# A two-layer diffusion backbone on one core: the MLPs with six banks, another order of stores, loads and norms, and one more product straight to x

## The chip, the cores and the metric

The kernel runs on one core of a Trainium2 chip. The metric is the device time of one execution in microseconds, the median of several runs.

## The reference

A block of 1024 latent tokens `x` and 256 context tokens `ctx`, 1024 channels wide, go through two layers. Layer 0 is a mixer (Fourier and a state space scan), layer 1 differential attention. Each is followed by an MLP of width 4096. The part that matters here:

```python
def rmsnorm(x, g):
    xf = x.astype(F32)
    y = xf * lax.rsqrt(jnp.mean(xf * xf, axis=-1, keepdims=True) + EPS)
    return (y * g.astype(F32)).astype(x.dtype)

def modulate(h, shift, scale):
    return h * (1.0 + scale) + shift

def adaln(cond, w, b):
    m = jax.nn.silu(cond) @ w + b
    return jnp.split(m[..., None, :], 6, axis=-1)

def sq_relu_mlp(h, w1, w2):
    return jnp.square(jax.nn.relu(h @ w1)) @ w2

# in layer i, behind the mixer or the attention
x = x + g2 * sq_relu_mlp(modulate(rmsnorm(x, norm2_g[i]), sh2, sc2), mlp_w1[i], mlp_w2[i])
if not last:
    ctx = ctx + cg2 * sq_relu_mlp(modulate(rmsnorm(ctx, norm2_g[i]), csh2, csc2), mlp_w1[i], mlp_w2[i])
```

Layer 1 has no MLP for the context. Its modulations `adaln` need a product with a 1024 x 6144 matrix `ada_w`, once for the latent condition and in part for that of the context.

## The kernel before

All of x stays in SBUF with channels on partitions (`xL` for the 1024 latent tokens, `xC` for the context). Tokens are worked in three blocks: columns 0 to 511 and 512 to 1023 of the latents (named by 0 and 512) and the context (`SEQ`, 256 columns). Every fp32 operand of a product is kept as a high and a low half, made by `split` (L337: ACT casts the high half, POOL or DVE subtracts for the low one); `mm3` (L341 to L343) adds three matmuls, high by high, high by low, low by high.

**Products with w1** (`up`). The 32 column groups f of w1 are streamed (`Stream`, loads at L149 on SP's queue into a ring R of raw tiles, splits by ACT and POOL). A product of one f and one block is 8 x 3 matmuls into one PSUM bank, taken in turn from `self.bank(0, 1)`. ACT then reads the bank with relu (L1581) and squares in place. Two neighbouring f make a pair u. When all blocks of a pair are there, `results` makes seven combinations for a seven-product scheme of 2 x 2 blocks (and one for the context): T = C12 - C11 on DVE in a buffer E, then others; each is split by `keep` into a place of the buffer M and stored to DRAM (`h_w`, L1539, SP's queue). `keeps`, called at k = 0, 3 and 6 of each product, takes one step of it. The blocks of the last pair, f = 30 and 31, are taken in the order 0, 512, SEQ.

**Background work.** `self.step(n)` after each product takes n steps of a queue of generators. In the first MLP the queue holds `ada_dve(1)`: 24 chunks of 256 columns of layer 1's `ada_w`. A chunk is loaded in two tiles into ring R (L544, SP's queue), DVE multiplies and adds 8 k-slices into Y (line L296 for all fused operations; 16 operations for the first 8 chunks, which serve both conditions, then 8), and TensorE sums over the partitions (L526). `self.flush()` ends what is left.

**Products with w2.** For c of 0 to 6, q of 0, 1, j of 0 to 6, two products with combined weights (`down_weights`, made on DVE, ACT and POOL), with operands fetched back from `h_w` into slots by POOL's queue (L1604). Products j = 1, 5, 6 go from the bank straight to x by `to_x`, x += gate * bank. The others (0, 2, 3, 4) are summed over c in M by DVE; at c = 6, `together` combines them with POOL additions and adds to x. The last pair of w1 groups, u = 14 and 15 of w2, is multiplied plainly (`last`): block 0 and the context for each d, and then block 512.

**Norms.** `hook(t0, n, d, i)` is called when a channel tile d of a block is final. For a block in `at_once` it squares on ACT and sums on DVE or POOL at once; for others it is done later, in the steps between. The sum over partitions is at L392, its spreading over the partitions at L406. The projections of the attention follow the first MLP, with operands `hl` (latents) and `hc` (context).

In the second MLP there are only two blocks, no `ada` work, and four result places in M.

## Time and profile before

| | |
|---|---|
| median of 3 runs | 3011.8 us (3011.11 to 3018.55) |
| profiled execution | 3013.48 us, span 3011.7 us |
| PE busy | 2815.6 us, 93% |
| DVE busy | 1967.2 us, 65% |
| POOL busy | 1559.2 us, 52% |
| ACT busy | 1131.9 us, 38% |
| DMA | 504.58 MB, mean 168 GB/s |
| mean granted clock of TensorE | 0.97 |

The times in the rows are counted from the start of the span. The products with w1 of the first MLP lie at about 490 to 1055 us, those with w2 until about 1480, the attention's projections from 1492. The second MLP runs from about 2333 to the end. A line number with an engine is the line of the code that issued the instruction; many DVE operations go through one helper (L296), so the operands' names tell them apart. A wait is put down to the engine and line that released it last.

### The profile page before, as it was taken

The numbers are of one execution on the slowest core, as the hardware profiler recorded it, in microseconds if no ns is written. First come the engines' busy times: TensorE is split into PE (matmuls) and PEld (weight loads), VectorE is DVE, ScalarE is ACT, GpSimd is POOL, SyncE is SP. The second block draws the span as 40 slices with busy tenths as digits, with TensorE's granted clock in tenths as the row PEclk, the third lists the DMA queues.
The fourth block names the chain that finished last, engine by engine and source line by source line (L and its number), as shares of the span: only waits on it lengthen the run. The fifth ranks groups of instructions, "written<-read, shape, count | busy, mean of one in ns | idle before, by whom it ended". The sixth has DMA issues, their size and how long they took to land.

```text
span 3011.7 us, 40545 instructions
## 1 busy us (share of the span) xinstructions
PE 2815.6 (93%) x14850; PEld 2342.4 (78%) x14850; DVE 1967.2 (65%) x3694; ACT 1131.9 (38%) x2036; POOL 1559.2 (52%) x1282
## 2 busy tenths in 40 slices
PE   5899999888888889999789999999999999999999
PEld 2666788777777778888667878999988888877887
DVE  7889877555333445557648893999986543446666
ACT  3342343333333321111323443666653544532220
POOL 5613233433343465667524442777751555667775
PEclk8898999999999899999999999999999999999999
DMA  7265530555555785856126454232313465589882
GB/s 288 85 188 167 193 102 8 189 182 199 206 203 204 245 248 172 254 170 196 60 97 168 131 136 136 84 95 76 109 36 119 148 235 203 222 278 290 251 248 82
DMA packets 304358, 504.58 MB, mean 168 GB/s; under 512 B 17568, under 2 KB 175776, under 8 KB 303648
## 3 DMA queue, kind: packets, MB, share of 16 engines
q1 hardware_dynamic: 235344, 355.18, 35.4%
q0 software_dynamic: 68816, 146.82, 16.3%
q8 instruction: 117, 1.92, 0.3%
q14 instruction: 81, 0.66, 0.1%
HBM read 332.56 MB, written 169.38 MB: 167 GB/s over the span
## 4 chain that ended last, share of the span: by engine, by line
PE 68%; DVE 12%; DMA 7%; issue 5%; ACT 4%; POOL 3%; SPq 0%; DVEq 0%; POOLq 0%; ACTq 0%
PE bank L341 17%; PE bank L343 16%; PE bank L342 16%; DMA R<-in_ada_w_dram 4%; PE sc L1957 4%; PE pv L1997 4%; DVE Y L296 4%; PE tb L1988 2%; DVE E L296 2%; DVE S L296 1%; PE sc L342 1%; PE sc L343 1%; PE sc L341 1%; POOL M L337 1%; DVE hl L296 1%
## 5 line engine op out<-in xcount | busy, mean ns | idle before, releaser
L337 POOL TENSOR_TENSOR W<-R,W 128x512 fp32r<-128x512 f32 (+1 forms) x196 | 341.1, 1750 | 509.9 <-ACT W L333 501.9
L341 PE MATMUL bank<-hl,W 128*128 128x512 f32 (+1 forms) x1224 | 490.7, 401 | 70.2 <-ACT M L1581 61.5
L342 PE MATMUL bank<-hl,W 128*128 128x512 f32 (+1 forms) x1224 | 482.4, 394 | 5.5 <-DVE hl L296 5.5
L343 PE MATMUL bank<-hl,W 128*128 128x512 f32 (+1 forms) x1224 | 479.9, 392 | 1.0 <-DVE W L337 1.0
L341 PE MATMUL bank<-hb,W 128*128 128x512 f32 x968 | 381.8, 394 | 3.2 <-ACT W L333 1.7
L343 PE MATMUL bank<-hb,W 128*128 128x512 f32 x968 | 379.7, 392 | 1.3 <-POOL W L337 1.3
L342 PE MATMUL bank<-hb,W 128*128 128x512 f32 x968 | 377.4, 390 | 0.0
L341 PEld LDWEIGHTS bank<-hl,W 128*128 128x128 f32 x1224 | 238.3, 195 | 141.8 <-ACT M L1581 64.4
L333 ACT CAST W<-R 128x512 fp32r<-128x512 f32 (+2 forms) x237 | 184.7, 798 | 303.2 <-PE bank L343 157.3
L342 PEld LDWEIGHTS bank<-hl,W 128*128 128x128 f32 x1224 | 238.3, 195 | 52.9 <-DVE hl L296 9.8
L343 PEld LDWEIGHTS bank<-hl,W 128*128 128x128 f32 x1224 | 237.2, 194 | 50.2 <-DVE W L337 1.4
L296 DVE SCALAR_TENSOR_TENSOR xL<-bank,k,xL 128x512 f32<-128x512 f32 x232 | 171.6, 747 | 133.5 <-PE bank L343 130.3
L296 DVE SCALAR_TENSOR_TENSOR Y<-R,k,Y 128x256 f32<-128x256 f32 x224 | 152.4, 713 | 102.2 <-DMA R<-in_ada_w_dram 99.0
L343 PEld LDWEIGHTS bank<-hb,W 128*128 128x128 f32 x968 | 182.0, 188 | 43.5 <-POOL W L337 2.1
L341 PEld LDWEIGHTS bank<-hb,W 128*128 128x128 f32 x968 | 182.2, 188 | 43.0 <-ACT W L333 2.5
L342 PEld LDWEIGHTS bank<-hb,W 128*128 128x128 f32 x968 | 182.2, 188 | 40.0 <-issue 0.2
L1962 DVE TENSOR_REDUCE S<-sc 128x1 f32<-128x1280 f32 x128 | 184.2, 1479 | 38.9 <-PE sc L1957 38.9
L296 DVE TENSOR_TENSOR M<-bank,M 128x512 f32<-128x512 f32 x192 | 131.2, 689 | 105.5 <-PE bank L343 105.4
L337 POOL TENSOR_TENSOR W<-E,W 128x512 fp32r<-128x512 f32 x112 | 144.9, 1312 | 98.6 <-ACT W L333 98.4
L1581 ACT ACTIVATE M<-bank 128x512 f32<-128x512 f32 (+1 forms) x160 | 88.4, 553 | 264.4 <-PE bank L343 264.3
L1957 PE MATMUL sc<-K,W 128*128 128x512 f32 x720 | 168.1, 370 | 0.0
L324 POOL TENSOR_TENSOR R<-R,S 128x896 f32<-128x896 f32 x64 | 107.3, 1677 | 111.2 <-DVE S L296 94.2
(405 smaller groups left out, 6488.5 us busy)
## 6 DMA issues: line engine op xcount, KB each, us to landing
h_w<-M SPq DMA_DIRECT2D x228, 512.0 KB, 3.1
hl<-h_w POOLq DMA_DIRECT2D x106, 512.0 KB, 7.5
hb<-h_w POOLq DMA_DIRECT2D x106, 512.0 KB, 7.7
R<-in_w_dram SPq DMA_DIRECT2D x64, 512.0 KB, 4.1
R<-in_w_dram SPq DMA_DIRECT2D x112, 256.0 KB, 4.6
R<-in_ada_w_dram SPq DMA_DIRECT2D x52, 512.0 KB, 4.3
W<-q_d POOLq DMA_DIRECT2D x15, 1024.0 KB, 5.4
A<-in_ada_w_dram SPq DMA_DIRECT2D x24, 512.0 KB, 4.7
```

The lines of the kernel that those rows point to most:

```text
L296: f(**kw)
L324: self.nc.gpsimd.tensor_tensor(out=o, in0=a, in1=b, op=op)
L333: nc.scalar.copy(hi, src)
L337: e.tensor_tensor(out=lo, in0=src, in1=hi.bitcast(F32), op=ALU.subtract)
L341: mm(ps, lhsT=lh, rhs=rh, start=first, stop=False)
L342: mm(ps, lhsT=lh, rhs=rl, start=False, stop=False)
L343: mm(ps, lhsT=ll, rhs=rh, start=False, stop=last)
L1581: nc.scalar.activation(out=e, in_=ps, func=AF.Relu)
L1957: nc.tensor.matmul(self.SC[i][:, c0:c0 + n], lhsT=Qf[:, e, q0:q0 + 128], rhs=K[:, i, c0:c0 + n], start=e == 0, stop=e == 1)
L1962: nc.vector.tensor_reduce(out=st[:, i, 1:2], in_=self.SC[i][:, 0:1280], axis=AX.X, op=ALU.max, negate=True)
L1988: nc.tensor.transpose(ps[:, 128 * j:128 * j + 128], it["P"][0][:, 128 * (c0 + j):128 * (c0 + j) + 128], self.ident)
L1997: nc.tensor.matmul(self.PV[:, 0:128], lhsT=it["wT"][:, kt], rhs=heads[h]["v"][:, kt], start=kt == 8, stop=kt == 3)
```

## The change

Both MLPs are changed, by parts:

- `up` takes its bank from six in turn, not two.
- A store of a result is issued one `keep` later (`held`).
- `Stream.lean`, set in the first MLP: after a split the next raw load is issued only if none is waiting.
- `step` after a product takes 2 and 3 steps in turn.
- The last pair's blocks are taken in the order SEQ, 0, 512 in the first MLP, and the context's first operands are fetched right behind the context's products.
- For the plainly multiplied pair, every second split of w2 has its subtraction on DVE.
- Product j = 4 goes straight to x twice (512 of d and of 4 + d); M needs 12 places, `together` two additions.
- At the end of the first MLP the context's `hook` comes after that of block 512, and block 512's squares are summed at once.
- The second MLP has three result places; its x-hat of block 512 lies in `oS`, whose other half gives 8 free slots, and Y serves for a part of M (`Halves`).

```diff
 class Stream:
-        self.extra, self.depth, self.turn = [], 2, 0
+        self.extra, self.depth, self.turn, self.lean = [], 2, 0, False
...
-        self.load()
+        if not self.lean or self.nl <= self.ns:
+            self.load()
...
-                self.split(a, w[:, 0].rearrange("p a b -> p (a b)"), w[:, 1].rearrange("p a b -> p (a b)"), elo="p")
+                self.split(a, w[:, 0].rearrange("p a b -> p (a b)"), w[:, 1].rearrange("p a b -> p (a b)"),
+                           elo="v" if u > 13 and i % 2 else "p")
...
-        turn = ([10, 12, 14] if ctx else [8, 10, 12, 14]) * 50
+        turn = ([10, 12, 14] if ctx else [8, 10, 12]) * 50
...
+        held = []
...
-                t = turn.pop(0) if u < 15 else (12, 14)[i % 2]
-                o = duo(t)
+                o = duo(turn.pop(0) if u < 15 else ((12, 14) if ctx else (12, 10))[i % 2])
                 self.split(src, o[:, 0].bitcast(F32R), o[:, 1].bitcast(F32R), elo=elo)
-                nc.sync.dma_start(out=fl(hd)[u, i], in_=o.rearrange("p a b -> p (a b)"))
+                if held:
+                    held.pop(0)()
+                held.append(lambda: nc.sync.dma_start(out=fl(hd)[u, i], in_=o.rearrange("p a b -> p (a b)")))
...
         def up(f, w, t0, n, beside):
-            ps, (hh, hl), u = self.bank(0, 1)[:, :n], self.hv(t0, n), f // 2
+            ps, (hh, hl), u = self.bank(0, 1, 2, 3, 4, 5)[:, :n], self.hv(t0, n), f // 2
...
-            self.step(2)
+            count[2] += 1
+            self.step(2 + count[2] % 2)
...
             if k % 3 == 0 and done:
                 if next(done[0], 0) == 0:
                     done.pop(0)
+            elif k % 3 == 0 and held:
+                held.pop(0)()
...
-        free = [None]
-        for t0, n in blocks:
+        free, last_up = [None], blocks[2:] + blocks[:2]
+        for t0, n in last_up:
...
-            if t0 != blocks[-1][0]:
+            if t0 == SEQ:
+                fetch_ctx(0)
+            elif t0 == 0:
                 fetch_free(*free)
         self.ws.done(2)
         make(6)
-        fetch_ctx(0)
         fetch_free(*free)
...
-        M = [{(0, 0): 0, (0, 1): 1, (2, 0): 2, (2, 1): 3, (3, 0): 8, (3, 1): 9, (4, 0): 10, (4, 1): 11},
-             {(0, 0): 4, (0, 1): 5, (2, 0): 6, (2, 1): 7, (3, 0): 12, (3, 1): 13, (4, 0): 14, (4, 1): 15}]
+        M = [{(0, 0): 0, (0, 1): 1, (2, 0): 2, (2, 1): 3, (3, 0): 8, (3, 1): 9},
+             {(0, 0): 4, (0, 1): 5, (2, 0): 6, (2, 1): 7, (3, 0): 10, (3, 1): 11}]
+        TO = {1: [(0, 0)], 4: [(0, 512), (4, 512)], 5: [(0, 512)], 6: [(4, 0)]}
...
-                        if j in (1, 5, 6):
-                            to_x(ps, dh if j == 6 else dl, 512 if j == 5 else 0)
+                        if j in TO:
+                            for d, t0 in TO[j]:
+                                to_x(ps, d + 2 * q + e, t0)
...
                 last(w, d, t0, n)
-                hook(t0, n, d, i)
+                if t0 < SEQ:
+                    hook(t0, n, d, i)
...
+            for i, d in enumerate(self.LAST):
+                hook(SEQ, CTX, d, i)
...
-        hook = self.norm_hook(1, 0, pool=True, wait=(3, 3))
+        hook = self.norm_hook(1, 0, (0, 512), pool=True, wait=(3, 3))
...
+        self.ws.lean = True
         self.mlp(0, MIX, slots, sc, ready, hook, before)
+        self.ws.lean = False
...
-        slots = [(None, hb2.v(6, 2, 512)[:, i]) for i in range(6)] + [(0, v0[:, :, i]) for i in range(8)] + \
-                [(512, v1[:, :, i]) for i in range(8)]
+        slots = [(t0, a[:, :, i, o:o + 512]) for t0, a, o in ((None, oS, 512), (0, v0, 0), (512, oS, 0))
+                 for i in range(8)]
```

Three places of the new order follow. The numbers behind a name are those of its buffers; a line of the changed kernel is 16 to 29 higher than the same one before.

TensorE at the end of the w1 products of the first MLP. Before, the last context product of f = 29, four sums over the partitions of ada chunks, and the first product of the last pair:

```order
L343 MATMUL bank1_1_61<-hc_50_3828,W12_53_7688 128x256
L526 MATMUL bank1_7_67<-k_7_94,Y53_21_7899 128x1 x2
L526 MATMUL bank1_7_67<-k_7_94,Y53_22_7998 128x1 x2
L526 MATMUL bank1_7_67<-k_7_94,Y53_23_8014 128x1 x2
L526 MATMUL bank1_7_67<-k_7_94,Y53_24_8030 128x1 x2
L341 MATMUL bank1_0_60<-hl_47_3675,W12_54_7782 128x512
```

Changed, the last of all these sums, six products earlier than there (W12_51 is the weight of f = 27, W12_52 that of f = 28):

```order
L359 MATMUL bank1_5_65<-hc_50_3828,W12_51_7539 128x256
L542 MATMUL bank1_7_67<-k_7_94,Y53_24_7720 128x1 x2
L357 MATMUL bank1_0_60<-hl_47_3675,W12_52_7637 128x512
L358 MATMUL bank1_0_60<-hl_47_3675,W12_52_7637 128x512
L359 MATMUL bank1_0_60<-hl_47_3675,W12_52_7637 128x512
```

The last sum has moved in front of f = 28's products, and no sum stands between the loop and the last pair.

POOL's queue around the last product with w1, before (hl_47 and hl_48 are slots of block 0 and 512, hc_50 those of the context; W12 are weights for w2):

```order
L1604 DMA hl_47_3675<-h_w0_4555 128x2x512 x6
L1604 DMA hl_48_3679<-h_w0_4555 128x2x512 x4
L1604 DMA hl_47_3675<-h_w0_4555 128x2x512 x2
L1604 DMA hl_48_3679<-h_w0_4555 128x2x512 x4
L337 TENSOR_TENSOR W12_57_8255<-E14_189_8059,W12_57_8255 128x512
L337 TENSOR_TENSOR W12_57_8255<-E14_190_8060,W12_57_8255 128x512
L337 TENSOR_TENSOR W12_58_8261<-E14_188_8058,W12_58_8261 128x512
L337 TENSOR_TENSOR W12_58_8261<-E14_189_8059,W12_58_8261 128x512
L1604 DMA hc_50_3828<-h_w0_4555 128x2x512 x4
```

Changed:

```order
L1627 DMA hc_50_3828<-h_w0_4555 128x2x512 x2
L1627 DMA hl_47_3675<-h_w0_4555 128x2x512 x6
L353 TENSOR_TENSOR W12_57_8247<-E14_189_8059,W12_57_8247 128x512
L353 TENSOR_TENSOR W12_57_8247<-E14_190_8060,W12_57_8247 128x512
L353 TENSOR_TENSOR W12_58_8253<-E14_188_8058,W12_58_8253 128x512
L353 TENSOR_TENSOR W12_58_8253<-E14_189_8059,W12_58_8253 128x512
L1627 DMA hl_48_3679<-h_w0_4555 128x2x512 x4
L1627 DMA hl_47_3675<-h_w0_4555 128x2x512 x2
L1627 DMA hl_48_3679<-h_w0_4555 128x2x512 x4
L1627 DMA hc_50_3828<-h_w0_4555 128x2x512 x2
```

The first two fetches of hc have moved from behind the four splits of W12 to the front, and the fetches into hl_48 from in front of the splits to behind them.

DVE at the end of the first MLP, where Y53 holds the sums of squares (256 columns for the context, 512 for a latent block) and the writes of xL are the last products' additions to x. Before:

```order
L337 TENSOR_TENSOR hl_47_3675<-E14_243_11395,hl_47_3675 128x512
L296 SCALAR_TENSOR_TENSOR hl_47_3675<-E14_244_11413,k_9_102,hl_47_3675 128x512
L296 TENSOR_TENSOR Y53_28_11419<-Y53_28_11419,E14_245_11421 128x256
L296 SCALAR_TENSOR_TENSOR xL_37_2870<-bank1_2_62,k_9_102,xL_37_2870 128x512
L296 TENSOR_TENSOR Y53_28_11419<-Y53_28_11419,E14_246_11442 128x256
L296 TENSOR_TENSOR Y53_28_11419<-Y53_28_11419,E14_247_11445 128x256
L296 TENSOR_TENSOR Y53_28_11419<-Y53_28_11419,E14_248_11448 128x256
L296 TENSOR_TENSOR Y53_28_11419<-Y53_28_11419,E14_249_11451 128x256
L296 TENSOR_TENSOR Y53_28_11419<-Y53_28_11419,E14_250_11454 128x256
L296 TENSOR_TENSOR Y53_28_11419<-Y53_28_11419,E14_251_11457 128x256
L296 SCALAR_TENSOR_TENSOR xL_37_2870<-bank1_3_63,k_9_102,xL_37_2870 128x512
```

Changed:

```order
L312 SCALAR_TENSOR_TENSOR E14_249_11447<-xL_37_2870,k_10_106,Y53_28_11356 128x512
L353 TENSOR_TENSOR hl_47_3675<-E14_247_11426,hl_47_3675 128x512
L312 SCALAR_TENSOR_TENSOR hl_47_3675<-E14_249_11447,k_9_102,hl_47_3675 128x512
L312 SCALAR_TENSOR_TENSOR xL_37_2870<-bank1_2_62,k_9_102,xL_37_2870 128x512
L312 TENSOR_TENSOR Y53_27_11295<-Y53_27_11295,E14_248_11445 128x512
L312 SCALAR_TENSOR_TENSOR xL_37_2870<-bank1_3_63,k_9_102,xL_37_2870 128x512
L312 TENSOR_TENSOR Y53_27_11295<-Y53_27_11295,E14_250_11472 128x512
L312 TENSOR_TENSOR Y53_27_11295<-Y53_27_11295,E14_251_11488 128x512
L353 TENSOR_TENSOR W12_122_11491<-R13_153_11456,W12_122_11491 128x512 x2
```

The last addition to xL has come ahead of the context's sums, which no longer stand here; sums of block 512 stand in their place, one ahead of it and two behind.

## Rows read from the trace of the kernel before

**Rows 1.** Busy time of each engine by stage; then granted clock, DMA share, GB/s.

```profile
490.00:1080.00 590.00, 508.23 (x2532) 432.67 (x2531) 276.92 (x469) 211.44 (x373) 240.73 (x170) 0.92 0.56 193
1080.00:1440.00 360.00, 357.48 (x1903) 308.81 (x1902) 215.68 (x315) 68.80 (x116) 242.81 (x234) 1.00 0.68 202
1440.00:1560.00 120.00, 93.25 (x403) 73.15 (x404) 67.37 (x119) 38.22 (x70) 49.05 (x38) 0.89 0.17 52
```

**Rows 2.** Waits of PE, 480 to 1090: total us, times, longest us.

```profile
PE bank L341 <- ACT M L1581: 63.6, 16, 6.5
PE bank L341 <- DMA hc<-h_w: 9.5, 2, 9.2
PE bank L526 <- DVE Y L296: 8.8, 4, 3.4
```

**Rows 3.** Timeline of PE after a wait: start, us, what [idle before <-releaser].

```profile
726.38 0.79 PE L341 MATMUL bank<-hl,W 128*128 128x512 f32 x1 [4.57 <-ACT M L1581]
726.97 0.63 PE L342 MATMUL bank<-hl,W 128*128 128x512 f32 x1
727.40 0.63 PE L343 MATMUL bank<-hl,W 128*128 128x512 f32 x1
...
733.57 0.40 PE L342 MATMUL bank<-hl,W 128*128 128x512 f32 x1
733.80 0.39 PE L343 MATMUL bank<-hl,W 128*128 128x512 f32 x1
```

**Rows 4.** Timeline of DVE around the same wait.

```profile
722.30 1.67 DVE L296 SCALAR_TENSOR_TENSOR Y<-R,k,Y 128x256 f32<-128x256 f32 x4 [4.62 <-DMA R<-in_ada_w_dram]
723.89 0.68 DVE L296 TENSOR_TENSOR E<-M,E 128x512 f32<-128x512 f32 x1
...
725.10 4.73 DVE L296 SCALAR_TENSOR_TENSOR Y<-R,k,Y 128x256 f32<-128x256 f32 x4
```

**Rows 5.** Timeline of ACT around the same wait.

```profile
724.65 0.62 ACT L333 CAST M<-E 128x512 fp32r<-128x512 f32 x1 [6.16 <-DVE E L296]
...
725.74 0.59 ACT L1581 ACTIVATE M<-bank 128x512 f32<-128x512 f32 x1
```

**Rows 6.** Timeline of POOL around the same wait.

```profile
725.35 1.35 POOL L337 TENSOR_TENSOR M<-E,M 128x512 fp32r<-128x512 f32 x1 [5.49 <-ACT M L333]
```

**Rows 7.** Waits of DVE, 480 to 1060: total us, times, longest us.

```profile
DVE Y L296 <- DMA R<-in_ada_w_dram: 206.0, 41, 9.1
```

**Rows 8.** Busy time of DVE, 560 to 750.

```profile
560.00:750.00 190.00, 107.06 (x172) 0.92 0.56 196
```

**Rows 9.** Timeline of POOL at the end of the w1 stage.

```profile
1056.32 5.41 POOL L337 TENSOR_TENSOR W<-E,W 128x512 fp32r<-128x512 f32 x4 [0.41 <-ACT W L333]
1061.67 2.87 POOL L1604 DMA_DIRECT2D hc<-h_w  x4
```

**Rows 10.** Waits of PE, 1080 to 1560.

```profile
PE bank L341 <- DVE xL L296: 14.3, 2, 12.9
PE bank L341 <- ACT hl L333: 5.3, 3, 4.1
PE bank L406 <- DVE E L296: 4.2, 2, 3.0
PE bank L392 <- DVE Y L296: 2.7, 1, 2.7
PE bank L341 <- DVE M L296: 1.5, 2, 0.8
```

**Rows 11.** Timeline of DVE at the end of the first MLP.

```profile
1485.85 4.47 DVE L296 TENSOR_TENSOR Y<-Y,E 128x256 f32<-128x256 f32 x5
...
1491.12 0.74 DVE L296 SCALAR_TENSOR_TENSOR xL<-bank,k,xL 128x512 f32<-128x512 f32 x1
```

**Rows 12.** Waits of PE in the second MLP's w1 stage, 2330 to 2690.

```profile
PE bank L341 <- ACT M L1581: 1.5, 1, 1.5
```

**Rows 13.** Waits of ACT in that same stage.

```profile
ACT M L333 <- DMA h_w<-M: 33.0, 28, 3.0
```

More of the change, by code (lines that the diff above doesn't have):

```diff
@@ L95, in v, with __init__, free @@
         return self.places.pop(0)
+class Halves:
+    def __init__(self, b):
+        self.b, self.i = b, 1
+    def v(self, *shape):
+        self.i ^= 1
+        return self.b.v(*shape, o=self.b.n // 2 * self.i)
+    def free(self):
+        self.b.free()
 class Alt:
@@ L1505, in mlp @@
         ctx = len(order) == 3
-        mem = [self.buf("M", 6144)]
+        mem = [self.buf("M", 6144, side="L" if ctx else "R")]
         def duo(i):
@@ L1516, in mlp @@
         fl = lambda a: a.bitcast(F32)
-        turn = ([10, 12, 14] if ctx else [8, 10, 12, 14]) * 50
+        turn = ([10, 12, 14] if ctx else [8, 10, 12]) * 50
         total = (14 * 8 + 16) if ctx else (14 * 7 + 8)
-        gen, Wq, count = self.down_weights(layer, ctx, 1 + ctx), [], [0, -1]
+        gen, Wq, count = self.down_weights(layer, ctx, 1 + ctx), [], [0, -1, 0]
         def make(k=1):
@@ L1668, in together @@
             q, e = divmod(dp, 2)
-            m = {j: place(M[q][j, e]) for j in (0, 2, 3, 4)}
+            m = {j: place(M[q][j, e]) for j in (0, 2, 3)}
             to_x(m[0], dp, 0)
@@ L1673, in together @@
             self.ptt(m[3], m[2], m[3], ALU.add)
+            to_x(m[2], dp, 512)
             yield
             to_x(m[3], dp + 4, 0)
-            self.ptt(m[2], m[2], m[4], ALU.add)
             yield
-            to_x(m[2], dp, 512)
-            self.ptt(m[4], m[3], m[4], ALU.add)
-            yield
-            to_x(m[4], dp + 4, 512)
+            to_x(m[3], dp + 4, 512)
             yield
@@ L1706, in mlp @@
                     for e in range(2):
-                        ps, dl, dh = bank(), 2 * q + e, 4 + 2 * q + e
+                        ps = bank()
                         for p in range(2):
@@ L1728, in mlp @@
                         keeps(0)
+                        if j == 6:
+                            while done or held:
+                                keeps(0)
                     if c == 6 and q:
@@ L1754, in mlp @@
             self.go(g)
-        for r in mem:
+        for r in mem[:1 + ctx]:
             r.free()
@@ L2153, in hook @@
                 if i == 0:
-                    acc[t0] = [self.Y.v(n) for _ in range(2 if pool else 1)]
+                    acc[t0] = [self.Y.v(n) for _ in range(2 if pool and t0 == 0 else 1)]
                 for add in left.pop(t0, []):
@@ L2328, in second @@
         self.Kr.free()
[L2329 to L2331 removed]
+        hb0 = b("hb0", 2 * 8 * 512, True)
+        v0, v1 = hb0.v(2, 8, 512), oS[:, :, :, 0:512]
+        self.hx_views([v0[:, 0], v0[:, 1]], [v1[:, 0], v1[:, 1]])
         for _ in gen:
             pass
[L2334 to L2337 removed]
         self.ws.eng = ("a", "p")
@@ L2343, in put @@
             nc.sync.dma_start(out=self.out[:, d, t0:t0 + n], in_=self.xL.v(8, SEQ)[:, d, t0:t0 + n])
-        slots = [(None, hb2.v(6, 2, 512)[:, i]) for i in range(6)] + [(0, v0[:, :, i]) for i in range(8)] + \
-                [(512, v1[:, :, i]) for i in range(8)]
+        slots = [(t0, a[:, :, i, o:o + 512]) for t0, a, o in ((None, oS, 512), (0, v0, 0), (512, oS, 0))
+                 for i in range(8)]
         self.mlp(1, LAT, slots, (), None, put, lambda t0, n: self.flush_norm(t0))
-        for h in (hb2, hb1, self.Y, hb0):
+        for h in (hb0, self.Y, oSb):
             h.free()
```

11 lines of the change are left out of this document (2 added, 9 removed).

## The prediction

> **What bounds the kernel now.** I first read the busy shares by stage [rows 1], because the mean over the program hides where TensorE stands still. From 490 to 1080 us (first MLP, products with w1) PE is busy 508.23 of 590 us at a mean granted clock of 0.92. In the products with w2 that follow, 1080 to 1440, it is busy 357.48 of 360 at 1.00. From 1440 to 1560, the end of that MLP and the start of the attention projections, it is busy 93.25 of 120 at 0.89. In the other MLP, PE waits 1.5 us in all of its w1 stage [rows 12], with the same two banks. So there are two holes, some 82 us of waiting and some 27, each with a slow clock beside it. The rest that the change touches runs at TensorE's pace.
>
> Next I read who is waited for. In the first hole: 63.6 us in 16 waits for ACT's relu of an earlier product (its bank isn't read yet), 9.5 for the fetch of hc, 8.8 in four waits for the sums of the ada steps [rows 2]. That is 81.9, the whole hole. One of the 16 shows the chain [rows 3 to 5]. DVE gives E, the difference that ACT must cast, at 723.89; ACT casts it at 724.65 after 6.16 us of waiting, and the relu that PE needs stands behind it on ACT's queue and runs at 725.74. PE starts at 726.38, 4.57 us late. So the relus aren't slow (0.59 us). They queue behind a cast that waits for DVE, and with two banks PE can be only one product ahead. DVE is late since it waits for the ada weights, 206.0 us in 41 waits [rows 7], in order with the rest of its work.
>
> After that wait PE's starts lie 0.43 us apart (726.97 to 727.40), later 0.23 (733.57 to 733.80) [rows 3]: the two clock levels, 1.2 and 2.4 GHz. The clock was at the lower one when PE came out of the wait.
>
> **Six banks in the w1 stage.** A 512-column product is 24 matmuls x 0.23 = 5.5 us. PE may now run five products ahead instead of one, so ACT may be 4 x 5.5 = 22 us later than before without PE noticing. The longest wait was 6.5 [rows 2], three in a row would still fit, and ACT, busy 211.44 of 590 us [rows 1], catches up. Gone: 63.6, less about 5 (estimated) for the first of the 16, where the block's norm, whose making isn't changed, would be late next. Gain 58.6; at least 37 if ACT's delays add up and the 22 us are won only once.
>
> **Ada steps denser.** `step` is called with 2 or 3 per product instead of 2; most of the sums on PE now come every third product instead of every fourth. The four sums that stood behind the loop, 8.8 us [rows 2], come before its end: gain 8.8. But DVE must do a chunk in less time. The stretch 560 to 750 holds 8 chunks of 16 operations with DVE busy 107.06 [rows 8]. About 24 of the 190 us are PE's waits (the hole's 13% share) and 15 its clock of 0.92, so the same PE work lasts about 151. It then carries 10.7 chunks. A step takes 0.42 or 1.18 us (below), 0.73 with POOL busy 41% of the time [rows 1]; 107.06 + 2.7 x 16 x 0.73 = 139 of 151 us, 92% of DVE. PE waits for a sum directly, so lateness is now a gap. DVE in time gives 0; the longest wait of this kind before, 3.4 us [rows 2], on each of the eight heavy chunks gives 27. I take 14. The other 16 chunks have half the operations, and PE's products hide them; without that cover they cost as much again, 14.
>
> Four fused ada steps took 1.67 us at 722.30 with POOL idle, and 4.73 at 725.10 with POOL at work from 725.35 [rows 4, 6]: 0.42 against 1.18 each. The Trainium skill (GPSIMD Engine Reference, 1. Specifications) says that GpSimd shares its SBUF interfaces with VectorE and contends with VectorE instructions that have two SBUF inputs. By that rule DVE work packed closer beside the same POOL work gets dearer, and the time would be rival 2's; the trace agrees on the mechanism, and not yet on the amount.
>
> **Last pair by blocks, fetch of hc early.** hc's fetch stood behind four POOL splits of weights (5.41 us from 1056.32), was issued at 1061.67 [rows 9], and PE waited 9.2 [rows 2]. It is now issued ahead of them, after the context's products, whose buffer it takes: 9.5 gone. Late next are the operands of j = 3, whose fetch now stands behind the same four splits, so at about 1061.7. PE gets to j = 3 after six products of 6 x 0.23 us and four context parts of half that, 11 us. The old wait met PE some 3 us after its last w1 product, this one 8 us later with the same issue time. Between 0 and the old 9.2 I take 4. Net 5.5.
>
> **The clock.** 590 us at 0.92 is 47 us of full-clock work lost [rows 1], over 21 waits or so. I count nine waits left (the norm, seven at ada sums, j = 3), so 47 x 12/21 = 27 would return; part of the slow time lay inside the waits and is counted already, so I take 20, from 10 to 40.
>
> The Trainium skill (TensorE: Matmul & The Clock Gate, A second HAM failure mode: psum-queue depth-cycling) speaks against this: in one kernel, cycling through PSUM banks in each iteration let the clock swing, which is rival 5 here. The w2 stage cycles through six banks at 1.00 and the w1 stage swings with two [rows 1], so the trace doesn't bear it out.
>
> **Order at the end of the MLP.** The first projection waits 12.9 us for a bank that DVE's last addition to x frees [rows 10]. That addition, 1491.12, stands on DVE behind six sums of the context's norm, from 1485.85 on [rows 11]. They move behind it: 1491.12 - 1485.85 = 5.3 gained. The waits of 5.3, 4.2 and 2.7 [rows 10] belong to the second block's norm, which came behind the context's and now comes first; I leave 4 of these 12.2, gain 8.2. j = 4 no longer adds to M, so the 1.5 for M [rows 10] goes too. The clock of 0.89 lost 13 of 120 us [rows 1]; with about half of the waits gone I take 5. Sum 20, from 7 (only the bank) to 30.
>
> **Work put on DVE.** j = 4 goes to x twice and leaves M: 56 more fused additions of 0.74 [rows 11] are at most 41 us over the w2 stage, less the additions to M that go. DVE is busy 215.68 of 360 there [rows 1], PE's products hide it, and I take 0; it costs what goes over 360, so nothing even at the full 41. Eight w2 splits moved from POOL to DVE at the end are as short; at worst they delay an addition by 0.7 us each, 6.
>
> **Second MLP.** PE waits 1.5 us in its w1 stage [rows 12], so nothing is to be won. Three result places instead of four and stores one result later can cost: ACT waits 33.0 us in 28 for a store to leave its place [rows 13]. Four more banks lie ahead of that; I take 0, between -1.5 and 20. The later stores, the w1 load asked for only when needed (first MLP) and x-hat's new home put no wait on PE's own queue; the loads stand on SP's, and a late one shows as DVE's wait for ada weights (rival 4).
>
> **Sum.** 58.6 + 8.8 - 14 + 5.5 + 20 + 20 = 98.9. The profiled execution took 3013.5 us, so 2914.6; it lies 1.7 above the median of the three runs (3011.8), so 2913.
>
> **Rivals.**
> 1. *All is hidden.* DVE keeps up, j = 3 isn't late, the clock returns whole for these waits: 14 + 4 + 13 more, 2882. For it: DVE idles 83 of the 190 us [rows 8]. Against: 92% of an engine that works in order.
> 2. *DVE sets the pace in the first w1 stage.* With POOL beside it three quarters of the time a step takes 0.99, a chunk 15.8, and with 1.3 of results 17.1 against 14.1 of PE work: 3.0 late on each of 8 chunks, 24 rather than 14, and the clock's 20 doesn't return: 2943.
> 3. *Banks only postpone.* If ACT's lateness is a rate, 22 are won once and 36.6 stay, the clock keeps half, and the sums' 14 fall away: 2946. Against: ACT's share of 36%.
> 4. *Slower.* DVE's 206.0 us of waits for ada weights [rows 7] reached PE only in part. With sums a third closer and SP's queue in another order they could reach it whole, in place of the 14: 2913 + 192 = 3105. It decides from 113 (14 + 99) of the 206: there the gain is gone. Against: two slots are left to these loads, and part of the wait is time with nothing due.
> 5. *The clock stays at 0.92* with the waits gone: 2933.
>
> **Chances.** Forecast 0.52; rival 1 0.14, 2 0.15, 3 0.08, 4 0.05, 5 0.02; 0.04 that several mishaps make it level. A difference of 0.3% (9 us) is about what a measurement of this kernel can tell from no change. Faster 0.91, same 0.04, slower 0.05. The range goes from 2872 (rival 1 with the tail at its best) to 2962 (rivals 2 and 3 with the tail's 20 at 7).
>
> **What would show it.** In the changed profile: no waits of PE for ACT's relu between 540 and 1000; the sums' waits for DVE between 0 and 27 us; the stage's clock at 0.96 or more; no wait for hc, a short one for hl at j = 3; the first projection waiting 7 to 8 us. More than 30 us at the sums mean rival 2 or 4, more than 20 us behind ACT rival 3. I am wrong at the root if the w1 stage is hardly shorter though its waits for ACT are gone.

## The result

The changed kernel takes 2933.9 us in the median of four runs (2931.0 to 2938.3), against 3013.7 for the kernel before beside it. The ratio is 0.9735, with a 95% interval from 0.9715 to 0.9754: about 80 us faster. The forecast was 2913 with a range of 2872 to 2962. The profiled execution took 2932.1 us, its span 2930.3.

The busy times by stage of the changed kernel come first (columns as in [rows 1]; this kernel's stages lie earlier, so the windows do too):

```profile
490.00:1020.00 530.00, 503.75 (x2593) 429.74 (x2592) 283.95 (x478) 212.98 (x373) 240.58 (x170) 0.98 0.62 214
1080.00:1360.00 280.00, 280.00 (x1487) 242.13 (x1486) 185.41 (x276) 53.47 (x90) 181.37 (x179) 1.00 0.71 208
1380.00:1500.00 120.00, 105.11 (x458) 85.70 (x457) 71.68 (x123) 39.61 (x69) 43.99 (x33) 0.93 0.27 88
```

In the w1 stage PE is now busy 95% (503.75 of 530) where it was 86%, and the clock stands at 0.98 where it was 0.92 [rows 1]. The w2 stage is full, as before. The passage to the attention is at 105.11 of 120 and 0.93, from 93.25 of 120 and 0.89.

Next the waits of PE in the w1 stage and at the entry of w2 (total us, times, longest):

```profile
PE bank L542 <- DVE Y L312: 21.3, 9, 5.0
PE bank L357 <- ACT W L349: 5.1, 1, 5.1
PE bank L358 <- DVE hl L353: 2.4, 3, 1.4
PE bank L357 <- DMA hl<-h_w: 1.4, 3, 0.8
PE bank L359 <- POOL W L353: 0.8, 1, 0.8
```

No line for the relu is left, where [rows 2] had 63.6 us, and none for hc. PE waits for the sums of the ada steps, 21.3 us instead of 8.8, and at the entry of the w2 products, about 1026 us, it waits 5.1 us for the cast of a weight, which the forecast didn't have.

To place the rest, time was read at fixed counts of PE's matmuls. Every kernel here issues 14,850 of them; the 2,600th lies at the start of the w1 stage, the 5,300th in the first w2 products, the 7,450th in the projections, the 13,480th at the end of the second MLP's w1 stage, the 13,800th in its w2 products. The work between two of these is the same but for its order, in which the same shapes of matmuls stand.

| us from matmul to matmul | before | changed | difference | forecast |
|---|---|---|---|---|
| 2,600 to 5,300: w1 stage, entry of w2 | 618.7 | 555.2 | -63.5 | -78.9 |
| 5,300 to 7,450: w2, tail, projections | 456.6 | 438.4 | -18.2 | -20 |
| 7,450 to 13,480: attention, second w1 stage | 1106.6 | 1101.1 | -5.5 | 0 |
| 13,480 to 13,800: entry of the second w2 stage | 77.5 | 85.0 | +7.5 | 0 |
| 13,800 to the end | 245.3 | 242.8 | -2.5 | 0 |

The forecasts in the last column are those of the prediction's sum; for the first stage 58.6 + 8.8 - 14 + 5.5 + 20 = 78.9. So the missing part lies in the first stage. Whether its terms are right can't be read from the total; the experiments take it apart.

### The profile page after: what moved, and what is told of

Same layout as the page of the kernel before. It is cut to its first block, busy times and chain, and to the rows that moved or that the text cites. A ratio compares the mean times of both kernels' runs of the same rounds, so it can differ in the third digit from the quotient of the medians.

```text
span 2930.3 us, 40649 instructions
## 1 busy us (share of the span) xinstructions
PE 2789.2 (95%) x14850; PEld 2330.0 (80%) x14850; DVE 2005.3 (68%) x3762; ACT 1134.1 (39%) x2036; POOL 1521.7 (52%) x1254
## 4 chain that ended last, share of the span: by engine, by line
PE 67%; DVE 14%; DMA 7%; issue 5%; ACT 3%; POOL 3%; SPq 0%; POOLq 0%; ACTq 0%; DVEq 0%
PE bank L357 17%; PE bank L359 17%; PE bank L358 17%; PE sc L1986 4%; PE pv L2026 4%; DVE T L923 2%; PE tb L2017 2%; DMA h_w<-M 2%; DVE E L312 2%; DVE xh L927 2%; DMA R<-in_ada_w_dram 2%; DVE Y L312 2%; POOL W L353 1%; POOL M L353 1%; DVE S L312 1%
## 5 line engine op out<-in xcount | busy, mean ns | idle before, releaser
L353 POOL TENSOR_TENSOR W<-R,W 128x512 fp32r<-128x512 f32 (+1 forms) x184 | 326.0, 1779 | 455.3 <-ACT W L349 454.2
L357 PE MATMUL bank<-hl,W 128*128 128x512 f32 (+1 forms) x1224 | 482.4, 394 | 12.7 <-ACT W L349 6.5
L358 PE MATMUL bank<-hl,W 128*128 128x512 f32 (+1 forms) x1224 | 477.4, 390 | 8.2 <-DVE hl L312 5.5
L359 PE MATMUL bank<-hl,W 128*128 128x512 f32 (+1 forms) x1224 | 474.0, 387 | 1.8 <-DVE W L353 1.0
L312 DVE SCALAR_TENSOR_TENSOR xL<-bank,k,xL 128x512 f32<-128x512 f32 x344 | 245.9, 746 | 109.9 <-PE bank L359 106.6
L357 PEld LDWEIGHTS bank<-hl,W 128*128 128x128 f32 x1224 | 234.1, 191 | 80.9 <-issue 20.6
L358 PEld LDWEIGHTS bank<-hl,W 128*128 128x128 f32 x1224 | 234.4, 192 | 56.4 <-DVE hl L312 11.4
L359 PEld LDWEIGHTS bank<-hl,W 128*128 128x128 f32 x1224 | 233.8, 191 | 50.0 <-POOL W L353 1.6
L357 PE MATMUL bank<-oS,W 128*128 128x512 f32 x568 | 222.2, 391 | 7.2 <-ACT W L349 6.7
L359 PE MATMUL bank<-oS,W 128*128 128x512 f32 x568 | 222.0, 391 | 0.9 <-POOL W L353 0.9
L358 PE MATMUL bank<-oS,W 128*128 128x512 f32 x568 | 221.9, 391 | 0.0
L359 PE MATMUL bank<-hb,W 128*128 128x512 f32 x400 | 155.7, 389 | 1.5 <-POOL W L353 1.5
L312 DVE TENSOR_TENSOR M<-bank,M 128x512 f32<-128x512 f32 x144 | 99.1, 691 | 84.1 <-PE bank L359 84.0
L357 PE MATMUL bank<-hb,W 128*128 128x512 f32 x400 | 156.2, 390 | 0.0
L2026 PE MATMUL pv<-xL,wT 128*128 128x128 f32 x1280 | 155.8, 275 | 0.0
```

Source lines behind the costliest of these rows:

```text
L312: f(**kw)
L353: e.tensor_tensor(out=lo, in0=src, in1=hi.bitcast(F32), op=ALU.subtract)
L357: mm(ps, lhsT=lh, rhs=rh, start=first, stop=False)
L358: mm(ps, lhsT=lh, rhs=rl, start=False, stop=False)
L359: mm(ps, lhsT=ll, rhs=rh, start=False, stop=last)
L2026: nc.tensor.matmul(self.PV[:, 0:128], lhsT=it["wT"][:, kt], rhs=heads[h]["v"][:, kt], start=kt == 8, stop=kt == 3)
```

## Experiments

Ratios are to the kernel before, timed beside each kernel on the same chip; 0.001 is 3.0 us. The row for the changed kernel is 0.9735. "Stage" is the time from the 2,600th to the 5,300th matmul in the profiled execution.

| kernel | median us | ratio (95%) | stage us |
|---|---|---|---|
| before | | 1 | 618.7 |
| six banks alone | 2993.8 | 0.9922 (0.9893 to 0.9950) | 606.2 |
| lean alone | 3002.9 | 0.9951 (0.9936 to 0.9966) | 607.5 |
| six banks and lean | 2973.1 | 0.9858 (0.9841 to 0.9875) | 577.3 |
| six banks, lean, held stores | 2946.8 | 0.9764 (0.9750 to 0.9779) | 544.3 |
| changed | 2933.9 | 0.9735 (0.9715 to 0.9754) | 555.2 |
| changed, two banks | 2951.8 | 0.9783 (0.9764 to 0.9801) | 566.5 |
| changed, not lean | 2976.6 | 0.9862 (0.9847 to 0.9877) | 597.9 |
| changed, stores not held | 2944.3 | 0.9763 (0.9745 to 0.9782) | 568.6 |
| changed, two steps per product | 2919.4 | 0.9682 (0.9662 to 0.9701) | 543.3 |
| changed, sums later | 2935.1 | 0.9722 (0.9706 to 0.9738) | not read |
| changed, old order of norms | 2950.5 | 0.9777 (0.9761 to 0.9793) | 556.8 |
| changed, old order of the last pair | 2932.7 | 0.9717 (0.9703 to 0.9732) | 557.8 |
| two steps, last stores not held | 2914.6 | 0.9658 (0.9644 to 0.9673) | 540.3 |

### Six banks alone

The kernel before with one line changed:

```diff
-            ps, (hh, hl), u = self.bank(0, 1)[:, :n], self.hv(t0, n), f // 2
+            ps, (hh, hl), u = self.bank(0, 1, 2, 3, 4, 5)[:, :n], self.hv(t0, n), f // 2
```

> The kernel before, with one edit: the products with w1 take their bank from six in turn instead of two. My theory: the 63.6 us of waits for ACT's relu go whole, the slow clock behind them goes with them, and the four flushed sums (8.8), the fetch of hc (9.2) and the tail stay. That is 60 + 15 = 75 us, so about 2939 against 3014 of before; PE's waits for the relu under 5 us. Rival (banks only postpone, ACT's lateness is a rate): 22 us are won once, some 35 us of waits for the relu stay, the time is 2965 to 2985.

Measured: 0.9922, 23.5 us by the ratio, 12 in the profiled execution. Neither forecast was right. Its four executions spread over 18 us (2983.5 to 3001.6) and the profiled one is the longest, so the 12.5 us of its stage can be less than the banks gave in the others. The waits of PE from 480 to 1070 us:

```profile
PE bank L526 <- DVE Y L296: 57.1, 15, 10.1
```

The wait for the relu is gone to the last microsecond, as the theory said, and 57.1 us of waits for sums stand where 8.8 had been [rows 2]; the granted clock from 490 to 1070 us stays at 0.92. The longest of the waits shows where it comes from. First SP's queue in this kernel, then DVE, ACT and POOL, then PE (start, us, what, idle before and its releaser; in a row of several stores the time holds SP's waits between them):

```profile
682.19 0.39 SPq L544 DMA_DIRECT2D R<-in_ada_w_dram  x1
684.09 14.48 SPq L1539 DMA_DIRECT2D h_w<-M  x5
698.66 0.39 SPq L544 DMA_DIRECT2D R<-in_ada_w_dram  x1
```

```profile
688.94 0.61 DVE L296 TENSOR_SCALAR Y<-R,k 128x256 f32<-128x256 f32 x2 [7.18 <-DMA R<-in_ada_w_dram]
...
690.26 0.68 DVE L296 TENSOR_TENSOR E<-M,E 128x512 f32<-128x512 f32 x1
...
702.96 7.36 DVE L296 SCALAR_TENSOR_TENSOR Y<-R,k,Y 128x256 f32<-128x256 f32 x8 [4.60 <-DMA R<-in_ada_w_dram]
```

```profile
691.02 0.63 ACT L333 CAST M<-E 128x512 fp32r<-128x512 f32 x1 [8.32 <-issue]
```

```profile
691.72 1.37 POOL L337 TENSOR_TENSOR M<-E,M 128x512 fp32r<-128x512 f32 x1 [7.66 <-ACT M L333]
```

```profile
709.97 1.86 PE L526 MATMUL bank<-k,Y 128*128 128x1 f32 x8 [10.07 <-DVE Y L296]
```

SP is held 14.48 us, from 684.09, at five stores of results, which wait for subtractions, four on POOL and the last on DVE. The load of the second tile of the chunk's ada weights is issued behind them, at 698.66. DVE has waited 4.60 us for it, starts at 702.96 and ends at 710.3; PE, which starts on the sums as the last of DVE's operations runs, has waited 10.07 us at 709.97. The chain is stores on SP, load, DVE, and then whoever needs DVE: with two banks ACT's cast and through it the relu, with six banks the sum. The banks only moved its last link.

The chain has no first link either. The stores were late because DVE was: it had waited 7.18 us for the chunk's first tile and gave E only at 690.26; ACT casts it at 691.02, POOL subtracts at 691.72 after 7.66 us of waiting, and SP's next store goes out behind that. So it is a circle: a late load makes DVE late, DVE makes the stores late, and the stores the next load. [rows 4 to 6] show the same steps from DVE to POOL before the change.

### Lean alone, and both

```diff
-        self.load()
+        if not self.lean or self.nl <= self.ns:
+            self.load()
...
+        self.ws.lean = True
         self.mlp(0, MIX, slots, sc, ready, hook, before)
+        self.ws.lean = False
```

> The kernel before, with one edit: in the first MLP the next w1 load is issued only if none is waiting (lean), so that two places of the ring R are free for ada weights. Theory S (the stalls begin at SP: ada weights land late, DVE waits for them, ACT's cast for DVE, PE for ACT): DVE's waits for ada weights fall from 206 to about 130 us, PE's waits for the relu from 64 to about 30, 40 us gained: 2965 to 2980. Theory B (two banks are the cause): under 10 us, 3005 or more. Slower if PE then waits for w1 itself.

Measured: 0.9951, 15 us by the ratio, 10 in the profiled execution. This is a miss of the theory as it was put: DVE's waits for ada weights stay, 203.7 us, and PE's for the relu fall only from 63.6 to 52.2:

```profile
PE bank L342 <- ACT M L1582: 52.2, 15, 5.7
```

The waits of SP's queue, first in the kernel before, then in this one:

```profile
SPq L1539 <- POOL M L337: 193.0, 80, 7.5
...
SPq L149 <- POOL W L337: 74.1, 19, 13.4
```

```profile
SPq L1540 <- POOL M L338: 278.8, 87, 10.7
...
SPq L149 <- POOL W L338: 13.4, 1, 13.4
```

SP no longer stands at w1 loads for POOL's splits (13.4 us, from 74.1), but at the stores it stands 278.8 us where it stood 193.0. The 60.7 us that are taken out of the queue in one place come back in the other, and more.

> The kernel before with both edits, six banks and lean. Alone, the banks gave 23 us in the median (12 in the profiled execution), since PE's waits for the relu turned into 57 us of waits for sums. Theory S: with ada weights earlier the waits for sums fall under 25 us, and both edits together give more than their sum: 2945 to 2955. If each takes the same wait away twice, the gain is that of lean alone.

The edits of the two together. Measured: 0.9858, 43 us, where the two alone give 38 by their ratios. The profiled executions are clearer: 41.4 us in the stage, against 12.5 and 11.2. The waits for sums fall from 57.1 to 38.0, not under 25, and the median of 2973.1 lies outside the 2945 to 2955 that theory S gave:

```profile
PE bank L527 <- DVE Y L297: 38.0, 16, 3.7
```

```profile
DVE Y L297 <- DMA R<-in_ada_w_dram: 171.2, 40, 10.1
```

### Banks, lean and held stores

To the last kernel the held stores are added, with the two places that issue what is still held (not shown), and nothing else of the change:

```diff
-                nc.sync.dma_start(out=fl(hd)[u, i], in_=o.rearrange("p a b -> p (a b)"))
+                if held:
+                    held.pop(0)()
+                held.append(lambda: nc.sync.dma_start(out=fl(hd)[u, i], in_=o.rearrange("p a b -> p (a b)")))
```

> The kernel before with six banks, lean and the stores issued one result later, nothing else of the change. Banks and lean together gave 1.4% (43 us). Theory S' (ada weights stand on SP's in-order queue behind stores that wait for POOL's subtraction; lean gives them places, holding the stores lets them pass): PE's waits for sums fall from 38 to about 22 us, DVE's waits for ada weights from 171 to about 140, another 10 to 18 us: 0.980 to 0.983 of before, with some us lost again where the second MLP passes to its w2 products. Rival (the stores on the queue don't matter): 0.985 to 0.987.

Measured: 0.9764, 71 us, more than expected. The waits of PE and of DVE:

```profile
PE bank L527 <- DVE Y L297: 16.3, 9, 3.7
```

```profile
DVE Y L297 <- DMA R<-in_ada_w_dram: 121.2, 42, 8.1
```

Held stores take PE's waits for sums from 38.0 to 16.3 and DVE's for ada weights from 171.2 to 121.2 us. The stage is down 74.4 us with three edits, of which the banks alone give 12.5 and lean alone 11.2 (the held stores weren't run alone). Between this kernel and the one before it only the place of the stores on SP's queue differs, and PE's waits for sums more than halve: that the order of stores and loads there makes over half of these waits is shown by it. SP itself still stands 238.1 us at the stores (263.9 with banks and lean): what changed is which loads stand behind them.

### Undone one at a time

Two banks again in the changed kernel:

> The changed kernel with two banks again in the products with w1, all else of the change kept. My theory: what the rest gives is the tail (18), the flush (9) and the entry into the w2 products (2), less longer waits for the relu since the ada steps come denser and ACT's cast stands longer behind DVE. 2985 to 3000. Rival: stores and loads placed later already free ACT and DVE, and the relu's waits fall below 35 us with two banks: 2950 to 2970.

Measured: 0.9783, 2951.8 us, so the rival was right, at the lower end of its 2950 to 2970: all the rest gives 65 us without the banks, and taking them away costs 14 by the ratio and 11.3 in the stage. The waits for the relu are 30.1 us, half of [rows 2]; ACT's casts of E wait 54.3 us for DVE between 480 and 1030, where they wait 122.1 in the kernel before:

```profile
PE bank L357 <- ACT M L1601: 30.1, 14, 7.4
```

Lean off in the changed kernel:

```diff
-        self.ws.lean = True
         self.mlp(0, MIX, slots, sc, ready, hook, before)
-        self.ws.lean = False
```

> The changed kernel without lean, all else kept. Theory S: DVE's waits for ada weights rise from 125 to about 200 us, PE's waits for sums from 21 to 50 or more: 2960 to 2975 against 2934. If the later stores do the work that I give to lean: under 2942.

Measured: 0.9862, 38 us lost. DVE's waits for ada weights rise from 125.3 to 180.6 us and PE's for sums from 21.3 to 52.7:

```profile
DVE Y L312 <- DMA R<-in_ada_w_dram: 125.3, 36, 10.1
```

```profile
DVE Y L312 <- DMA R<-in_ada_w_dram: 180.6, 46, 9.2
```

```profile
PE bank L542 <- DVE Y L312: 52.7, 12, 9.2
```

Stores not held in the changed kernel:

```diff
-                if held:
-                    held.pop(0)()
-                held.append(lambda: nc.sync.dma_start(out=fl(hd)[u, i], in_=o.rearrange("p a b -> p (a b)")))
+                nc.sync.dma_start(out=fl(hd)[u, i], in_=o.rearrange("p a b -> p (a b)"))
```

> The changed kernel with each store issued at once, not one result later. In the changed kernel ACT stands 21.4 us at the end of the first w1 stage and 19.4 us at the end of the second for a store to leave its place, a weight's cast behind it, and PE waits 6.0 and 7.5 us there. Theory A (the held store is stuck on SP's queue behind w2 loads): both waits go, 2920 to 2924. Theory B (the place is late for another reason, as three places are few): they stay, 2934. Theory C: without holding, SP stands at stores ahead of loads in the w1 stage, DVE's waits for ada weights rise from 125 us and PE's waits for sums from 21: over 2940.

Measured: 0.9763, 8 us lost (the two intervals overlap at their ends), which is theory A and theory C at once. In the stage 13.4 us are lost (568.6 against 555.2; waits for sums 30.1). At the entry of the second w2 stage 5.9 are won (79.1 against 85.0 from the 13,480th to the 13,800th matmul). What is won there is a wait that can be seen in the changed kernel at the end of its first w1 stage too. ACT, and SP's queue:

```profile
1025.15 0.62 ACT L349 CAST M<-M 128x512 fp32r<-128x512 f32 x1 [21.36 <-DMA h_w<-M]
1025.67 1.14 ACT L349 CAST W<-R 128x512 fp32r<-128x512 f32 x2
```

```profile
1014.09 1.20 SPq L1480 DMA_DIRECT2D R<-in_w_dram  x2
1015.35 1.58 SPq L1559 DMA_DIRECT2D h_w<-M  x2
```

```profile
SPq L1480 <- POOL W L353: 37.2, 1, 37.2
```

SP stands 37.2 us at a w2 load that waits for POOL, until 1014.09. The held store is behind it and goes out at 1015.35. Its place in M is what ACT needs for its next cast, at 1025.15, so ACT stands 21.36 us, and the weight's cast behind it at 1025.67 is the one for which PE waits 5.1 us. In the second MLP the same costs 6.7:

```profile
PE bank L357 <- ACT W L349: 6.7, 1, 6.7
```

### Two steps per product

```diff
-            count[2] += 1
-            self.step(2 + count[2] % 2)
+            self.step(2)
```

> The changed kernel with two background steps after every product, as before, instead of two and three in turn. The sums on PE come every fourth product again. My theory: of the 21.3 us that PE waits for sums about 15 go, the flush behind the loop comes back with 9 or so and its slow clock: 2926 to 2934, so little or no change against 2934. Rival (denser steps are the whole cost of the shortfall): 2915 or less. Rival (denser steps are a gain by themselves): over 2940.

Measured: 0.9682 against 0.9735, some 16 us faster than the changed kernel; in the stage 11.9 (543.3 against 555.2). The rival that blames the denser steps for the shortfall was nearer (2919.4, where it said 2915 or less). The sums that PE waits for:

```profile
PE bank L542 <- DVE Y L312: 15.4, 9, 3.9
```

```profile
941.59 0.61 PE L542 MATMUL bank<-k,Y 128*128 128x1 f32 x4 [1.34 <-DVE Y L312]
945.50 1.02 PE L542 MATMUL bank<-k,Y 128*128 128x1 f32 x4 [3.30 <-DVE Y L312]
950.37 1.01 PE L542 MATMUL bank<-k,Y 128*128 128x1 f32 x4 [3.85 <-DVE Y L312]
954.37 1.01 PE L542 MATMUL bank<-k,Y 128*128 128x1 f32 x4 [2.99 <-DVE Y L312]
```

Of the 15.4 us, 1.34 + 3.30 + 3.85 + 2.99 = 11.5 are the four flushed sums, which come back. So 3.9 are left for the whole loop, where the changed kernel has 21.3. Denser steps save 11.5 us of flush and cost 17.4 us of other waits. The other 6 of the 11.9 us aren't taken apart: the granted clock from 490 to 1020 us is 0.97 here and 0.98 in the changed kernel.

### Sums later

The sums of a chunk are put behind the first half of the next chunk's second tile, no longer behind its first tile (and taken into modc a step later):

```diff
-                if late and kh:
+                if chunk == 24 and kh:
                     place(late[0], late[2])
                     late = None
...
                     if k == 1:
+                        if late and kh:
+                            sums(late[1], late[2])
                         yield
                 yield
-                if late:
+                if late and chunk == 24:
                     sums(late[1], late[2])
+                if late and kh and chunk < 24:
+                    place(late[0], late[2])
+                    late = None
```

> The changed kernel with each chunk's sums on PE put half a chunk later, some 8 us of products behind their old place. If PE's 21 us of waits for sums are DVE's jitter, nearly all go, and their slow clock: 2905 to 2915. If DVE is the pace (it cannot do a chunk in three products), they only move: 2925 to 2934. If DVE comes to wait for PE, since a sum's buffer is freed later, PE waits no less: 2934 or more.

Measured: 2935.1 and 0.9722, whose interval (0.9706 to 0.9738) holds the 0.9735 of the changed kernel. So no gain that these runs can tell, and the first theory is out. The profiled execution took 15,682 us, for a reason that nothing here shows, and its rows are not used; the other three took 2933 to 2935. Which of the two other reasons holds, DVE as the pace or DVE waiting for PE, stays open.

### Order of norms, order of the last pair

The order of norms of before, in the changed kernel, which also puts off the squares and sums of block 512 again:

```diff
-                if t0 < SEQ:
-                    hook(t0, n, d, i)
+                hook(t0, n, d, i)
...
-            for i, d in enumerate(self.LAST):
-                hook(SEQ, CTX, d, i)
...
-                    acc[t0] = [self.Y.v(n) for _ in range(2 if pool and t0 == 0 else 1)]
+                    acc[t0] = [self.Y.v(n) for _ in range(2 if pool else 1)]
...
-        hook = self.norm_hook(1, 0, (0, 512), pool=True, wait=(3, 3))
+        hook = self.norm_hook(1, 0, pool=True, wait=(3, 3))
```

> The changed kernel with the order of norms of before at the end of the first MLP (the context's hook in the loop, block 512's squares summed later). If the order makes the gain there, the stage from the last w1 product to the end of the first projections is 16 to 20 us longer, 0.979 to 0.980 of before against 0.9735. Rival (it is the product j = 4 that left M, or the split of w2 on DVE): under 6 us longer.

Measured: 0.9777, 13 us lost by the ratio; from the 5,300th to the 7,450th matmul 452.4 us against 438.4, so 14.0 of the 18.2; somewhat under the 16 to 20 expected. The waits in the tail of this kernel, and of the changed one:

```profile
PE bank L357 <- DVE xL L312: 12.6, 1, 12.6
PE bank L357 <- ACT hl L349: 5.3, 3, 4.1
...
PE bank L408 <- DVE Y L312: 2.7, 1, 2.7
```

```profile
PE bank L357 <- DVE xL L312: 11.0, 1, 11.0
```

The waits of 5.3 and 2.7 are back as in [rows 10]; the wait for the bank is 12.6, and 11.0 in the changed kernel. So the order, with the sums made at once, makes most of the gain, and makes it in the waits of block 512's norm, and only 1.6 us of it in the bank's. Which of these two parts does it, no run tells.

The order of the last pair of before, in the changed kernel:

```diff
-        free, last_up = [None], blocks[2:] + blocks[:2]
-        for t0, n in last_up:
+        free = [None]
+        for t0, n in blocks:
...
-            if t0 == SEQ:
-                fetch_ctx(0)
-            elif t0 == 0:
+            if t0 != blocks[-1][0]:
                 fetch_free(*free)
         self.ws.done(2)
         make(6)
+        fetch_ctx(0)
```

> The changed kernel with the last pair's blocks in the order 0, 512, SEQ and the context's fetch at the end again. The wait for hc comes back with about 9 us; ACT's 21 us for a held store stand beside it, so PE's wait of 5.1 behind ACT falls into the same time, and the 2 us for hl of j = 3 go. Net 2 to 4 us longer: 0.974 to 0.975 of before. If the new order was worth its 5.5 us by itself: 0.9753 or more. Not longer: its gain was spent on the waits that it made.

Measured: 0.9717 (0.9703 to 0.9732), which overlaps the changed kernel's 0.9715 to 0.9754: not longer. The wait for hc is back, and the waits behind ACT, for hl and for POOL are not there:

```profile
PE bank L542 <- DVE Y L312: 23.7, 8, 7.4
PE bank L357 <- DMA hc<-h_w: 9.8, 2, 9.5
```

9.8 us stand against 5.1 + 1.4 + 0.8 = 7.3 in the changed kernel. What the new order gains is less than these runs can tell.

### A version that beats both

Two steps per product, as above, and the stores of the last pair issued at once:

```diff
-                held.append(lambda: nc.sync.dma_start(out=fl(hd)[u, i], in_=o.rearrange("p a b -> p (a b)")))
+                if u == 15:
+                    nc.sync.dma_start(out=fl(hd)[u, i], in_=o.rearrange("p a b -> p (a b)"))
+                else:
+                    held.append(lambda: nc.sync.dma_start(out=fl(hd)[u, i], in_=o.rearrange("p a b -> p (a b)")))
```

> A version meant to beat both: the changed kernel with two background steps after each product and with the stores of the last pair (u = 15) issued at once. Two steps gave 0.9682 of before against 0.9735. Without holding, PE's waits at the change to w2 in the second MLP fell by 6 us, and the cost of not holding lay in the w1 stage alone. Expected 0.966 to 0.967, some 4 to 7 us below two steps alone. If the stores at the end are late because of what stands ahead of them on SP, not because they are held: 0.968.

Measured: 2914.6 and 0.9658 (0.9644 to 0.9673), as expected: about 103 us below the kernel before and some 23 below the changed one. Against two steps alone it is 7 by the ratio, and those two intervals overlap. Its waits at the entry of the second w2 stage:

```profile
PE bank L359 <- POOL W L353: 4.5, 3, 3.0
```

The 6.7 us behind ACT are gone, and from the 13,480th to the 13,800th matmul it takes 79.6 us, against 85.0 in the changed kernel and 87.7 with two steps alone.

## Why the prediction was right, and where it was not

**The time.** 2933.9 lies in the range, and 21 us above the forecast. The sum was nearly right for a reason that was not: the largest term was too large by far, two terms that stood at nothing made up for most of it, and that was luck. Most of the signs that the prediction named for itself came true in the changed profile (no wait for the relu, 21.3 us at the sums, a clock of 0.98, none for hc and a short one for hl), because they tell which waits are gone and not which edit took them away. (The range's upper end, 2962, isn't quite what is named for it: rival 2 and rival 3 with the tail at 7 come to 2956 and 2959.)

**Six banks, 58.6: the step that failed.** Its claim was that ACT may be late without PE noticing. That holds: no wait for the relu is left. The step left out that DVE's lateness has a second way to PE. In the prediction's words, "DVE is late since it waits for the ada weights", and PE "waits for a sum directly"; the two were not put together. Alone, the banks gave 12 us in the profiled execution and 23 in the median, and the w1 stage was hardly shorter (606.2 from 618.7 us) though its waits for ACT were gone: the sign of being wrong at the root, met by the banks by themselves. In the stage they are worth 12.5 us alone, 30.2 beside lean (577.3 from 607.5) and 11.3 in the changed kernel. Rival 4 had this mechanism, with DVE's waits reaching PE, but took it for a danger of the denser steps and not as what the banks alone would meet. Rival 3 had the right effect, that banks postpone, and looked for it at the wrong place, since ACT's waits are gone. Rival 1 is out with 21.3 us of waits for sums.

**Stores and loads, 0: mis-sized.** They were said to put no wait on PE's own queue. They changed which loads stand behind which stores on SP's, where the circle passes: put on one after the other, the banks take 12.5 us off the stage, lean 28.9 more and the held stores 33.0 more; the rest of the change gives 10.9 back, and 63.5 are left. Taken out of the changed kernel, lean is worth 38 us by the ratio and holding the stores 8 net (13.4 won in the stage, 5.9 lost at the second entry). So a price depends on what else is in place, and these terms, put at 0, were worth more than the banks.

**Denser steps, 8.8 - 14: mis-sized.** 14 was taken from a range of 0 to 27; the waits for sums are 21.3. Half of them stand at the later chunks, which were taken as hidden:

```profile
PE bank L542 <- DVE Y L312: 11.5, 6, 2.9
```

The flush was worth 11.5 rather than 8.8 once PE no longer waits elsewhere. The part cost 11.9 in the stage where the sum had 5.2. The working by DVE's rate has two slips: the hole is 13.9% of the stage and not 13, and 2.5 steps per product with eight steps a chunk make 10.0 chunks in the same work, not 10.7; with both put right it gives 88% of DVE, not 92. Neither was borne out in the heavy stretch:

```profile
545.00:665.00 120.00, 75.77 (x141) 0.94 0.67 231
```

That is 63%, and DVE still waits 125.3 us in the stage for weights. In each of the nine chunks whose sum PE waits for, DVE had stood 3.0 us or more at a load of that chunk's weights. So a late load stands ahead of every one of these waits, where the working had DVE's rate. Rival 2 (steps dearer beside POOL) is not what happened, though the difference that it rests on is real [rows 4]: a fused step took 0.68 us in the mean between 545 and 690 (108 of them), where it took 0.77 before (107, between 560 and 750).

**Last pair, 5.5: not borne out.** The wait for hc went. In its place came 1.4 for hl, where 4 were allowed for j = 3, and 5.1 for a weight's cast behind a held store, which the prediction left out. Undone, nothing measurable changes.

**The clock, 20: right in kind.** The stage's clock is 0.98, where 0.96 or more was named, so rival 5 is out. It came back with the waits: with the banks alone, whose waits stayed, it is 0.92, with banks and lean 0.95, with the held stores 0.97 (490 to 1070 us). By the clock rows 47 us of full-clock work were lost before and 0.02 x 530 = 11 now. Part of that lay inside the waits, as the prediction said.

**The tail, 20: right, by another split.** 18.2 measured, 14.0 of it by the order of norms. The bank's wait fell only by 1.9 instead of 5.3, to 11.0 where 7 to 8 was named. What is late next on DVE was not looked for. The first projection in the changed kernel, and DVE's rows ahead of it:

```profile
1427.07 0.77 PE L357 MATMUL bank<-W,hl 128*128 128x512 f32 x1 [11.01 <-DVE xL L312]
```

```profile
1416.21 1.76 DVE L312 SCALAR_TENSOR_TENSOR E<-xL,k,Y 128x512 f32<-128x512 f32 x1
...
1423.06 0.74 DVE L312 SCALAR_TENSOR_TENSOR xL<-bank,k,xL 128x512 f32<-128x512 f32 x1
1423.72 2.54 DVE L312 TENSOR_TENSOR Y<-Y,E 128x512 f32<-128x512 f32 x1
1426.19 0.74 DVE L312 SCALAR_TENSOR_TENSOR xL<-bank,k,xL 128x512 f32<-128x512 f32 x1
```

The last product ended 11.0 us before 1427.07, at 1416.06. From there on DVE works off x-hat of block 0 and block 512's own sums, one of them 2.54 us long, before the last addition to x at 1426.19. The context's sums had been only one of the things that stood ahead.

**Second MLP, 0: right in total.** 5.5 won from the projections to the end of its w1 stage (3.5 of them in that stage, see the last section), 2.5 at the end, 7.5 lost at the entry of w2. The prediction's upper bound of 20 named the stores; what happened at the entry is a held store behind a w2 load, as in the first MLP.

## What to carry to other kernels

A wait that PE shows at a buffer need not begin there: follow it back until the engine that is late waits for a queue and not for work, and go on, for the queue can be waiting for that same engine. More buffers at the last link move such a wait to the next consumer; here they were worth 12.5 us of the stage alone, of 63.6 us of waits that they took away, and 30.2 beside an edit that changed the order of loads and stores on one queue. Of edits that share one chain, price them together, and test each alone and all but one.

## What was not expected of the hardware

In the second MLP's w1 stage, from the 12,000th to the 13,400th matmul, the changed kernel takes 317.3 us and the kernel before 320.8, though the profile lists no wait of PE between them in either. The difference is spread over the matmuls: the starts of two that follow each other are 226.7 ns apart in the mean, and 229.2 before. It isn't the number of banks. With six banks alone the same stretch takes 320.7 us and the median distance is 229 ns, as in the other kernels here that have the second MLP of before; with two banks in the changed kernel it takes 319.1, of which 1.2 are two waits for the relu, and the median distance is 227, as in all those read that have the changed second MLP. So the 3.5 us come with that part, its three result places and x-hat's new home among other moved buffers. Which of these does it, no run tells.
